# Gate stage of a hybrid encoder step: rows turned by VectorE, h added by accumulating loads, and rows finished one pair later

## The chip, the core and the metric

The kernel runs on one core of one Trainium2 chip. A core has five engines with their own instruction streams: TensorE (PE, its weight loads shown apart as PEld), VectorE (DVE), ScalarE (ACT), GpSimd (POOL) and SyncE (SP), which here only issues DMA transfers. POOL issues DMAs too, on a queue of its own. The metric is the device time of one launch in microseconds (us); lower is better. Traces give the span of one profiled execution from its first to its last instruction, and its own device time lies a little above that span.

## What is computed

2048 prompt frames and 32 frames of a running stream, D = 1024 channels in float32, go through one layer and a last norm:

```python
h = h + concat(yA, yB) @ w_out                       # "W_out stage"
gate = sigmoid(rmsnorm(h, g_ple) @ w_ple_gate)       # "gate stage"
h = h + (p @ w_ple) * gate
y = rmsnorm(h, g_final)                              # over the last axis, EPS = 1e-6
```

yA and yB come from one projection of rmsnorm(x), a short causal convolution and a multi-scale pooling; all of that lies ahead of the stages spoken of here and stays as it is. `rmsnorm(h, g)` is h / sqrt(mean(h*h) + EPS) * g. The kernel also returns states of the two mixers.

## The kernel before, in words

The program first makes yA and yB and leaves them in DRAM (`y_d`). The W_out stage reads them back, writes rows of h to DRAM (`h_d`) and the sums of squares of h to SBUF (`rs_h`, already turned into 1/rms). The product p @ w_ple is made beforehand for all but the very last tile and lies in DRAM (`e_d`). The gate weight, scaled by g_ple in `scale_gate` on ScalarE, lies in `g_d`.

The gate stage works on 17 row tiles: 16 of 128 prompt rows and a short one of 32. The short one goes first (`plain`), then eight pairs: seven in a loop, and `last_pair`, which has its own end. A pair is a 2 x 2 block product by a scheme of seven half-size products (`seven`): the left operand A is cut into A11, A12 (first tile of the pair, lower and upper half of the channels) and A21, A22 (second tile), with the sums S1 to S4 of them; the weight likewise (11, 12, 21, 22, T1 to T4). Each product is 12 matmuls, since float32 is carried as a high part and a low part in fp32r (hi*hi, hi*lo, lo*hi over four blocks of 128 channels). `split` makes the two parts: a cast on ScalarE, then a subtraction on VectorE. Three PSUM banks x, y, z of a pair hold the products, in this order: x 11, y 12, x S2, z S1, x S3, z S4, x 22. Between them `carry` copies the running sum of x or z out by ScalarE before the next product adds to it, and `out` turns a finished quarter into a gate: VectorE adds the carry, ScalarE takes the sigmoid with the row's 1/rms, VectorE multiplies by the tile e (L1324) and adds the result to the tile h (L1325).

While a pair runs, `prep_g` prepares A for the next one, in steps that are called between products. A needs channels on partitions, and `h_d` holds rows on partitions. Two ways stand in the code. `turned` (L1283) loads the rows as they are, ScalarE copies each half into another order of columns (L1291), TensorE turns it by four 128 x 128 transposes into PSUM (L1293). `turned_here` (L1297) loads the rows as blocks by four DMAs (L1302), and VectorE turns every 32 x 32 block in place (L1304). Before, the first tile of each pair goes the first way and the second tile the other. g_ple and the gate weight's rows are ordered to fit ("(q k c)").

When a pair's products are done, `done_g` (L1329) squares and sums a row on ScalarE (L88), makes 1/rms on POOL (L69, L73), scales on VectorE (L1332) and writes the rows to the output from POOL (L1333).

The order of instructions on each engine is set by a planner that sorts the program by estimated costs; `keep_in_program_order` ties an instruction to its place. Each engine works in order, so an instruction that waits holds up all behind it, DMA issues on SP and POOL too. Buffers come from rings (`tile_pool` with so many bufs): a new tile waits until the one that had its buffer is no longer read. Those that matter: `ya` (5 tiles of 128 x 1024: e, row loads), `xh` (3 of that size: h rows, gate weight rows), `qa` (before: 2 of 128 x 512), `ss` (3 of 128 x 512: the sums), `st` (4 of that size), `cmb` (8: the parts of A).

Of the kernel before, what the change touches and what calls it, by code (L numbers as in the profile page):

```python
# [22 lines left out]
PLE = 256  # L23
# [4 lines left out]
NH = D // 2  # L28
# [6 lines left out]
def trunk(ctx, tc, x_p, x_s, c_conv, c_pool, p_p, p_s, g_mix, w_in, conv_w, conv_b, pool_w,  # L35
# [271 lines left out]
    def ring4(t, name):  # L307
        return t.tile([P, D], F32, tag="t", name=name)
# [21 lines left out]
    with ExitStack() as s1:  # L330
# [17 lines left out]
        def put(piece, src):  # L348

            return split(piece[:, :, 0], piece[:, :, 1], src)  # L350
# [761 lines left out]
    with ExitStack() as s2:  # L1112
        pool = lambda name, bufs: s2.enter_context(tc.tile_pool(name=name, bufs=bufs, reuse_waits="tile"))
        w3, qa, xh, st, ss, cmb = (pool(*a) for a in (
            ("w3", 1), ("qa", 2), ("xh", 3), ("st", 4), ("ss", 3), ("cmb", 8)))

        def quarters(name, W):
            c = halves(slot(f"{name}_c"))
# [7 lines left out]
        def half_of(x, at, n=P):  # L1126
            return x[at[0]][:n, at[1] * NH:at[1] * NH + NH]
# [45 lines left out]
        def scale_gate(k):  # L1173

            ts = [qa.tile([P, NH], F32, tag="q", name=f"gs_{k}_{half}") for half in range(2)]
            rows = w_gate.rearrange("(q k c) n -> k q c n", q=4, k=KC)[k]
            for half, t in enumerate(ts):  # L1180
                nc.gpsimd.dma_start(t, rows[:, :, half * NH:half * NH + NH])
# [61 lines left out]
            next_gate()  # L1243


        def embedding_chunks(name):
            wp = []
            for k in range(2):
                raw = ring4(ya, f"{name}r_{k}")
# [33 lines left out]
        def turned(i):  # L1283

            r, n = tiles[i]
            t = load_rows(ya, "hn", i, h_d).rearrange("p (q k c) -> p k q c", q=4, k=KC)
            out = []
            for half in range(2):
                pt = tbank(f"pth_{i}_{half}")
                o = qa.tile([P, KH, P], F32, tag="q", name=f"ho_{i}_{half}")  # L1290
                nc.scalar.copy(o[:n].rearrange("p k (q c) -> p k q c", q=4), t[:n, half * KH:half * KH + KH])  # L1291
                for k in range(KH):
                    nc.tensor.transpose(pt[:, k * P:k * P + n], o[:n, k], ident[:n, :n])  # L1293
                out.append(pt.rearrange("p (k t) -> p k t", k=KH))
            return out

        def turned_here(i):  # L1297

            r, n = tiles[i]
            t = ring4(ya, f"hn_{i}")  # L1300
            for q in range(4):
                nc.sync.dma_start(t[q * 32:q * 32 + 32].rearrange("p (g c) -> p g c", g=4),  # L1302
                                  h_d[r:r + P, q * 256:q * 256 + 256].rearrange("(g p) c -> p g c", p=32))
            nc.vector.transpose(t, t)  # L1304
            u = t.rearrange("p (g k t) -> p k g t", g=4, k=KC)
            return u[:, :KH], u[:, KH:]

        def gate_ops(h, e, n, name, i):
            scale = lambda at: rs_h[:n, i + at[0]:i + at[0] + 1]

            def carry(ps, at):
                t = st.tile([P, NH], F32, tag="t", name=f"c_{name}_{at[0]}{at[1]}")
                nc.scalar.copy(t[:n], ps[:n])
                return t

            def out(ps, c, at):
                if c is None:
                    c = st.tile([P, NH], F32, tag="t", name=f"g_{name}_{at[0]}{at[1]}")
                    nc.scalar.activation(c[:n], ps[:n], AF.Sigmoid, scale=scale(at))
                else:  # L1320
                    nc.vector.tensor_tensor(c[:n], ps[:n], c[:n], op=ALU.add)
                    nc.scalar.activation(c[:n], c[:n], AF.Sigmoid, scale=scale(at))
                ee, hh = half_of(e, at, n), half_of(h, at, n)
                nc.vector.tensor_tensor(ee, ee, c[:n], op=ALU.mult)  # L1324
                nc.vector.tensor_tensor(hh, hh, ee, op=ALU.add)  # L1325

            return carry, out

        def done_g(i, h):  # L1329
            r, n = tiles[i]  # L1330
            rf = sumsq(h, n, f"f{i}")
            nc.vector.scalar_tensor_tensor(h[:n], h[:n], rf[:n], g_bc[:n], op0=ALU.mult, op1=ALU.mult)  # L1332
            nc.gpsimd.dma_start(rows_of(y_p, y_s, r, n), h[:n])  # L1333

        def short_ops(h, e, n):
# [17 lines left out]
        def last_pair(i, A):  # L1353
# [72 lines left out]
        def prep_g(i):  # L1426

            A = {}
            whole = lambda t: t.rearrange("p k (g t) -> p k g t", g=4)
# [7 lines left out]
                nc.vector.tensor_tensor(view(t), x, y, op=op)  # L1437
                return t

            lower = []  # L1440

            def first():
                lower.extend(turned_here(i + 1))

            def second():
                a21, a22 = lower
                s1 = comb("S1", a21, a22, ALU.add, whole)
                a11, a12 = turned(i)
                put("11", a11)
                s2 = comb("S2", s1, a11, ALU.subtract)  # L1450
                s3 = comb("S3", whole(a11), a21, ALU.subtract, whole)
                put("12", a12)
                put("S2", s2)
                s4 = comb("S4", a12, s2, ALU.subtract)
# [8 lines left out]
        S = {}  # L1463
        n = tiles[NT - 1][1]
        A = short("gl", turned(NT - 1), n)
        for step in prep_g(0).values():
# [5 lines left out]
        done_g(NT - 1, h)  # L1472
# [37 lines left out]
```

## Time and profile before

| | |
|---|---|
| median of 3 runs | 937.81 us (937.69 to 938.49) |
| the profiled execution: device time | 940.76 us |
| its span | 939.0 us |
| granted TensorE clock, mean | 0.992 |
| TensorE busy | 918.3 us, 98% of the span |
| VectorE busy | 727.4 us, 77% |
| ScalarE busy | 482.2 us, 51% |
| POOL busy | 129.3 us, 14% |
| gate stage, from the first pair's product to the end | 768.55 to 939.0 us |

How to read it: times are from the start of the span, in us unless marked ns. A group's line gives source line, engine, operation, output and input tile with shape, count, then busy time and the mean of one, then the idle time of the engine before it and what ended that. "The chain" is the work that ended last, followed back from the last instruction; each row is start, duration, engine, tile, line, count. Tile names are the program's; pth is the PSUM tile of the transposes, hn the row or block tile of h, ho the copy ahead of the transposes, g_S and g_fS the sums of A. Matmul durations overlap (389 ns each in a row, a new one every 227 ns).

### The profile page before, as it was taken

Reading aid. Unit: us, or ns where it says so; the run is one execution under the profiler, and the core shown is the slowest. Engines: PE = TensorE matmul, PEld = TensorE weight load, DVE = VectorE, ACT = ScalarE, POOL = GpSimd, SP = SyncE. Lnnn points to the kernel's source line nnn. Section 1 sums busy time; section 2 is a strip of 40 time slices with the busy share of each in tenths; the row PEclk is TensorE's granted clock in tenths of the full one; section 3 lists DMA queues with packets and bytes.
Section 4 is the critical chain, followed back from the end, with each engine's and each line's share of the span. In section 5 each row is a group of like instructions: output and inputs, shape, how many; then the busy total and the mean of one; then the engine's idle time right before and its main releaser. Section 6 shows DMA issues by size and latency. Waiting matters only on the chain.

```text
span 939.0 us, 13008 instructions
## 1 busy us (share of the span) xinstructions
PE 918.3 (98%) x4567; PEld 829.4 (88%) x4567; DVE 727.4 (77%) x1230; ACT 482.2 (51%) x894; POOL 129.3 (14%) x244
## 2 busy tenths in 40 slices
PE   6999999999999999999999999999999999999996
PEld 5899998999999999999999987888877868888885
DVE  6796898899588978685777589665554797888985
ACT  5653555464445554443444456334334875555663
POOL 2110232212000110000000010111211001211123
PEclk8999999999999999999999999999999999999998
DMA  8335556769955645427655359866785884566553
GB/s 240 85 121 175 154 146 203 222 174 297 417 167 139 180 142 166 129 71 272 195 167 175 128 187 289 270 181 183 218 244 171 318 264 129 206 220 244 183 207 113
DMA packets 133215, 182.97 MB, mean 195 GB/s; under 512 B 11164, under 2 KB 105116, under 8 KB 131869
## 3 DMA queue, kind: packets, MB, share of 16 engines
q1 hardware_dynamic: 117165, 131.70, 45.0%
q0 software_dynamic: 13248, 44.93, 14.6%
q10 hardware_dynamic: 2736, 5.51, 1.8%
q8 instruction: 36, 0.59, 0.3%
q14 instruction: 30, 0.25, 0.1%
HBM read 127.23 MB, written 54.86 MB: 194 GB/s over the span
## 4 chain that ended last, share of the span: by engine, by line
PE 79%; ACT 1%; DMA 1%; DVE 1%; POOL 0%; issue 0%; POOLq 0%; SPq 0%; ACTq 0%
PE x_o L167 9%; PE x_g L167 9%; PE x_zab L561 5%; PE x_ch L561 5%; PE x_zbv L561 5%; PE e L102 5%; PE z_g L167 5%; PE z_o L167 4%; PE z_ch L561 3%; PE z_zab L561 3%; PE z_zbv L561 2%; PE y_g L167 2%; PE y_o L167 2%; PE b L561 2%; PE za L561 2%; PE c L561 2%
## 5 line engine op out<-in xcount | busy, mean ns | idle before, releaser
L77 ACT CAST y_S<-y_fS 128x512 fp32r<-128x512 f32 x32 | 19.5, 621 | 43.1 <-PE x_o L167 19.4
L102 PE MATMUL e<-wq,pps 128*128 128x512 f32 (+1 forms) x156 | 38.8, 399 | 0.2 <-ACT pps L77 0.2
L406 DVE SCALAR_TENSOR_TENSOR xt<-xt,rstd_x,g_bc 128x1024 f32<-128x1024 f32 (+2 forms) x18 | 23.1, 1282 | 17.7 <-POOL rstd_x L73 17.5
L167 PE MATMUL x_g<-wg_b,g_S 128*128 128x512 f32 x128 | 35.9, 390 | 0.0
L167 PE MATMUL x_o<-wo_b,y_S 128*128 128x512 f32 x128 | 35.8, 391 | 0.0
L561 PE MATMUL x_zab<-B,w_zab_S 128*128 128x416 f32 x168 | 34.3, 352 | 0.5 <-ACT V L859 0.5
L561 PE MATMUL x_ch<-B,w_ch_S 128*128 128x416 f32 x168 | 34.6, 352 | 0.0
L561 PE MATMUL x_zbv<-B,w_zbv_S 128*128 128x416 f32 x168 | 34.4, 353 | 0.0
L561 PE MATMUL z_ch<-B,w_ch_S 128*128 128x416 f32 x168 | 34.1, 351 | 0.0
L561 PE MATMUL z_zbv<-B,w_zbv_S 128*128 128x416 f32 x168 | 34.1, 351 | 0.0
L561 PE MATMUL z_zab<-B,w_zab_S 128*128 128x416 f32 x168 | 34.0, 351 | 0.0
L102 PEld LDWEIGHTS e<-wq,pps 128*128 128x128 f32 (+1 forms) x156 | 27.4, 182 | 6.9 <-ACT pps L77 0.5
L561 PEld LDWEIGHTS x_zab<-B,w_zab_S 128*128 128x128 f32 x168 | 31.3, 188 | 1.1 <-ACT V L859 0.8
L561 PEld LDWEIGHTS x_zbv<-B,w_zbv_S 128*128 128x128 f32 x168 | 31.1, 188 | 0.8 <-ACT zs L859 0.4
L561 PEld LDWEIGHTS x_ch<-B,w_ch_S 128*128 128x128 f32 x168 | 31.2, 188 | 0.6 <-ACT c_s L859 0.3
L561 PEld LDWEIGHTS z_zab<-B,w_zab_S 128*128 128x128 f32 x168 | 31.4, 188 | 0.3
L561 PEld LDWEIGHTS z_ch<-B,w_ch_S 128*128 128x128 f32 x168 | 31.3, 188 | 0.4
L561 PEld LDWEIGHTS z_zbv<-B,w_zbv_S 128*128 128x128 f32 x168 | 31.3, 188 | 0.3
L69 POOL TENSOR_SCALAR ms_f<-ssq_f 128x1 f32<-128x1 f32 (+1 forms) x15 | 8.8, 588 | 160.7 <-ACT junk L88 160.7
L77 ACT CAST y<-y 128x512 fp32r<-128x512 f32 x24 | 14.8, 618 | 29.6 <-PE x_o L167 13.7
L1332 DVE SCALAR_TENSOR_TENSOR h<-h,rstd_f,g_bc 128x1024 f32<-128x1024 f32 (+1 forms) x15 | 19.3, 1284 | 12.7 <-POOL rstd_f L73 12.7
L167 PEld LDWEIGHTS x_o<-wo_b,y_S 128*128 128x128 f32 x128 | 24.0, 188 | 5.1 <-ACT c_o L1136 0.3
(571 smaller groups left out, 2670.4 us busy)
## 6 DMA issues: line engine op xcount, KB each, us to landing
y<-y_d SPq DMA_DIRECT2D x16, 512.0 KB, 12.8
x<-in_x_prompt_dram SPq DMA_DIRECT2D x16, 512.0 KB, 9.0
h_d<-x SPq DMA_DIRECT2D x16, 512.0 KB, 4.8
h<-h_d SPq DMA_DIRECT2D x16, 512.0 KB, 4.1
xt<-in_x_prompt_dram SPq DMA_DIRECT2D x15, 512.0 KB, 6.4
e<-e_d SPq DMA_DIRECT2D x15, 512.0 KB, 6.3
out_dram<-h POOLq DMA_DIRECT2D x14, 512.0 KB, 3.0
p_dT<-T POOLq DMA_DIRECT2D x12, 512.0 KB, 5.4
```

Source lines behind the costliest of these rows:

```text
L69: nc.gpsimd.tensor_scalar(ms[:n], ssq[:n], scalar1=1.0 / D, scalar2=EPS, op0=ALU.mult, op1=ALU.add)
L77: ins = nc.scalar.copy(hi, src)
L102: nc.tensor.matmul(ps[:n], pps[:, a, k, :n], wp[k][b][:, cs], start=k + q == 0, stop=k == 1 and q == 2)
L167: nc.tensor.matmul(ps[:n], lhs[:, k, a, :n], w[b][:, k], start=start and k + q == 0, stop=k == KH - 1 and q == 2, skip_group_check=True)
L406: nc.vector.scalar_tensor_tensor(xt[:n], xt[:n], r[:n], g_bc[:n], op0=ALU.mult, op1=ALU.mult)
L561: nc.tensor.matmul(ps[:, :NB], lhs[:, k, x], b[:, k, y], start=start and k + q == 0, stop=stop and k == KH - 1 and q == 2, skip_group_chec ...
L1332: nc.vector.scalar_tensor_tensor(h[:n], h[:n], rf[:n], g_bc[:n], op0=ALU.mult, op1=ALU.mult)
```

## The change

In the gate stage, for pairs two to eight, both tiles are loaded as blocks and turned by VectorE; the first pair's first tile still goes by TensorE. The block loads of the next pair are issued at the start of a pair, ahead of its loads of e. Their buffers are taken from `xh`, and from `qa` for every fourth tile. `qa` becomes one tile of 128 x 1024 instead of two of 128 x 512; in the W_out stage `scale_gate` takes the two halves of that tile.

The rows of h are no longer loaded in the loop. `out` ends with e times gate, and an accumulating DMA from POOL adds the rows of h from DRAM onto the tile e, half a tile at a time. So e becomes the new row, and it is finished one pair later: its sum of squares (`roots`) after the next pair's product z S1, its scaling and its output (`finished`) after x S3. The last pair still loads h, finishes the pair before it between its own products, and gets its buffers from `ss`, `xh` and `qa` instead of `ya`.

```diff
-            ("w3", 1), ("qa", 2), ("xh", 3), ("st", 4), ("ss", 3), ("cmb", 8)))
+            ("w3", 1), ("qa", 1), ("xh", 3), ("st", 4), ("ss", 3), ("cmb", 8)))
...
-            ts = [qa.tile([P, NH], F32, tag="q", name=f"gs_{k}_{half}") for half in range(2)]
+            gs = ring4(qa, f"gs_{k}")
+            ts = [gs[:, half * NH:half * NH + NH] for half in range(2)]
...
-        def turned_here(i):
+        def blocks(i):

             r, n = tiles[i]
-            t = ring4(ya, f"hn_{i}")
+            t = ring4(ya if i < 2 else qa if i % 4 == 1 else xh, f"hn_{i}")
             for q in range(4):
                 nc.sync.dma_start(t[q * 32:q * 32 + 32].rearrange("p (g c) -> p g c", g=4),
                                   h_d[r:r + P, q * 256:q * 256 + 256].rearrange("(g p) c -> p g c", p=32))
+            return t
+
+        def turned_here(t):
+
             nc.vector.transpose(t, t)
             u = t.rearrange("p (g k t) -> p k g t", g=4, k=KC)
             return u[:, :KH], u[:, KH:]
...
-                ee, hh = half_of(e, at, n), half_of(h, at, n)
+                ee = half_of(e, at, n)
                 nc.vector.tensor_tensor(ee, ee, c[:n], op=ALU.mult)
-                nc.vector.tensor_tensor(hh, hh, ee, op=ALU.add)
+                if h is None:
+                    r = tiles[i + at[0]][0]
+                    nc.gpsimd.dma_start(ee, h_d[r:r + P, at[1] * NH:at[1] * NH + NH], accum_op=ALU.add)
+                else:
+                    hh = half_of(h, at, n)
+                    nc.vector.tensor_tensor(hh, hh, ee, op=ALU.add)
...
-        def done_g(i, h):
+        def root_g(i, h, later=True):
+            return sumsq(h, tiles[i][1], f"f{i}", later=later)
+
+        def done_g(i, h, rf, later=True):
             r, n = tiles[i]
-            rf = sumsq(h, n, f"f{i}")
-            nc.vector.scalar_tensor_tensor(h[:n], h[:n], rf[:n], g_bc[:n], op0=ALU.mult, op1=ALU.mult)
+            ins = nc.vector.scalar_tensor_tensor(h[:n], h[:n], rf[:n], g_bc[:n], op0=ALU.mult, op1=ALU.mult)
+            if later:
+                tc.keep_in_program_order(ins)
             nc.gpsimd.dma_start(rows_of(y_p, y_s, r, n), h[:n])
...
-            pt = ring4(ya, "p_l")[:, :PLE]
+            pt = ss.tile([P, NH], F32, tag="s", name="p_l")[:, :PLE]
...
-            wp = embedding_chunks("wl")
+            wp = embedding_chunks("wl", (xh, qa))
...
-            seven(f"g{i}", A, W, carry, out, {5: lambda: second(1, NH)}, first_tile=True)
+            seven(f"g{i}", A, W, carry, out, {2: lambda: root(0), 3: lambda: (root(1), finished(0)), 4: lambda: finished(1), 5: lambda: second(1, NH)}, first_tile=True)
...
-            lower = []
+            rows = [blocks(i + b) for b in range(1 - here, 2)]
+            ready = []

             def first():
-                lower.extend(turned_here(i + 1))
+                ready.extend(turned_here(rows[0]))

             def second():
-                a21, a22 = lower
-                s1 = comb("S1", a21, a22, ALU.add, whole)
-                a11, a12 = turned(i)
-                put("11", a11)
...
+                if here:
+                    a11, a12 = ready
+                    put("11", a11, whole)
+                    a21, a22 = turned_here(rows[1])
+                    s1 = comb("S1", a21, a22, ALU.add, whole)
+                else:
+                    a21, a22 = ready
+                    s1 = comb("S1", a21, a22, ALU.add, whole)
+                    a11, a12 = map(whole, turned(i))
+                    put("11", a11, whole)
...
         for i in range(0, NT - 3, 2):
             A = S.pop(i)
-            h = [load_rows(xh, "h", i + b, h_d) for b in range(2)]
+            steps = prep_g(i + 2)
             e = [load_rows(ya, "e", i + b, e_d) for b in range(2)]
-            seven(f"g{i}", A, W, *gate_ops(h, e, P, f"g{i}", i), prep_g(i + 2))
-            for b in range(2):
-                done_g(i + b, h[b])
+            seven(f"g{i}", A, W, *gate_ops(None, e, P, f"g{i}", i), {**steps, 4: roots, 5: finished})
+            ready[:] = ([i + b, e[b]] for b in range(2))
         last_pair(NT - 3, S[NT - 3])
```

More of the change, by code (lines that the diff above doesn't have):

```diff
@@ L1287, in turned @@
             out = []
+            both = ring4(qa, f"ho_{i}").rearrange("p (h k t) -> p h k t", h=2, k=KH)
             for half in range(2):
                 pt = tbank(f"pth_{i}_{half}")
-                o = qa.tile([P, KH, P], F32, tag="q", name=f"ho_{i}_{half}")
+                o = both[:, half]
                 nc.scalar.copy(o[:n].rearrange("p k (q c) -> p k q c", q=4), t[:n, half * KH:half * KH + KH])
@@ L1422, in last_pair, with prep_g @@
             pps = embedded()
-            seven(f"g{i}", A, W, carry, out, {5: lambda: second(1, NH)}, first_tile=True)
+            seven(f"g{i}", A, W, carry, out, {2: lambda: root(0), 3: lambda: (root(1), finished(0)), 4: lambda: finished(1), 5: lambda: second(1, NH)}, first_tile=True)
             second(0, NH // 2)
-        def prep_g(i):
+        def prep_g(i, here=True):
             A = {}
@@ L1465, in trunk @@
         A = short("gl", turned(NT - 1), n)
-        for step in prep_g(0).values():
+        for step in prep_g(0, here=False).values():
             step()
@@ L1471, in trunk, with root, roots, finished @@
         plain("gl", A, W, n, *short_ops(h, e, n))
-        done_g(NT - 1, h)
+        done_g(NT - 1, h, root_g(NT - 1, h, False), False)
+        ready = []
+        def root(b):
+            ready[b].append(root_g(*ready[b]))
+        def roots():
+            for b in range(len(ready)):
+                root(b)
+        def finished(*bs):
+            for b in bs or range(len(ready)):
+                done_g(*ready[b])
         for i in range(0, NT - 3, 2):
             A = S.pop(i)
-            h = [load_rows(xh, "h", i + b, h_d) for b in range(2)]
+            steps = prep_g(i + 2)
             e = [load_rows(ya, "e", i + b, e_d) for b in range(2)]
-            seven(f"g{i}", A, W, *gate_ops(h, e, P, f"g{i}", i), prep_g(i + 2))
-            for b in range(2):
-                done_g(i + b, h[b])
+            seven(f"g{i}", A, W, *gate_ops(None, e, P, f"g{i}", i), {**steps, 4: roots, 5: finished})
+            ready[:] = ([i + b, e[b]] for b in range(2))
         last_pair(NT - 3, S[NT - 3])
```

12 lines of the change are left out of this document (6 added, 6 removed).

## The prediction

> **What bounds the kernel now.** I read the page first (busy times, the 40 slices), then the chain that ended last in order of time over the gate stage, then the busy times by stage, the groups of that stage, and its waits. The page:
>
> ```profile
> span 939.0 us, 13008 instructions
> PE 918.3 (98%) x4567; PEld 829.4 (88%) x4567; DVE 727.4 (77%) x1230; ACT 482.2 (51%) x894; POOL 129.3 (14%) x244
> PE   6999999999999999999999999999999999999996
> DMA  8335556769955645427655359866785884566553
> ```
>
> TensorE is busy in every slice but the first and the last, so a change pays only by what it takes off TensorE, or costs by what it makes TensorE wait for. The chain through the gate (start, us, line) shows what a pair of row tiles costs:
>
> ```profile
> 783.92 0.87 PE pth L1293 x8
> ...
> 785.94 5.44 PE x_g L167 x24
> ...
> 842.89 0.87 PE pth L1293 x8
> 843.76 2.06 PE z_g L167 x9
> 845.82 5.44 PE x_g L167 x24
> 851.26 2.72 PE y_g L167 x12
> 853.98 2.72 PE x_g L167 x12
> 856.70 2.72 PE z_g L167 x12
> 859.42 2.72 PE x_g L167 x12
> ...
> 901.55 0.87 PE pth L1293 x8
> ...
> 905.84 4.34 PE x_g L167 x19
> ```
>
> The chain never leaves TensorE: seven products of 12 matmuls, 2.72 us each, and one group of eight transposes (L1293), 0.87 us. From 785.94 to 905.84 lie six pairs and the last pair's transposes of p (0.22 us): (119.90 - 0.22) / 6 = 19.95 us a pair. Seven products are 7 x 2.72 = 19.05; 0.90 is left for the transposes with their seams. The stage and the tail (PE, PEld, DVE, ACT, POOL busy; clock; DMA share; GB/s):
>
> ```profile
> 785.90:905.84 119.94, 119.94 (x556) 99.75 (x555) 104.57 (x153) 69.64 (x122) 20.40 (x36) 1.00 0.59 205
> 905.84:939.00 33.16, 24.63 (x108) 19.82 (x107) 22.30 (x36) 16.40 (x31) 10.42 (x16) 0.91 0.32 120
> ```
>
> VectorE is at 104.57 / 119.94 = 87%, ScalarE at 58%, the DMA engines at 59%. No TensorE wait is in this window; what others wait for is small, or TensorE itself.
>
> **The change part by part.** Rows of the gate stage (count | busy us, mean ns):
>
> ```profile
> L1293 PE MATMUL pth<-ident,ho 128*128 128x128 f32 x48 | 6.4, 272 | 0.0
> L1291 ACT COPY ho<-hn 128x512 f32<-128x512 f32 x12 | 6.8, 622 | 0.0
> L77 ACT CAST g<-pth 128x512 fp32r<-128x512 f32 x12 | 6.5, 583 | 2.9 <-PE pth L1293 2.8
> L77 ACT CAST g<-hn 128x512 fp32r<-128x512 f32 x6 | 3.7, 618 | 0.0
> L1325 DVE TENSOR_TENSOR h<-h,e 128x512 f32<-128x512 f32 x24 | 15.9, 685 | 0.2
> L1304 DVE STREAM_TRANSPOSE hn<-hn 128x1024 f32<-128x1024 f32 x6 | 7.4, 1236 | 0.0
> L78 DVE TENSOR_TENSOR g_S<-g_fS,g_S 128x512 fp32r<-128x512 f32 x26 | 16.7, 681 | 0.2 <-ACT g_S L77 0.2
> L1332 DVE SCALAR_TENSOR_TENSOR h<-h,rstd_f,g_bc 128x1024 f32<-128x1024 f32 x12 | 15.4, 1285 | 10.0 <-POOL rstd_f L73 10.0
> L88 ACT ACTIVATE junk<-h 128x1024 bf16<-128x1024 f32 x12 | 12.7, 1058 | 11.5 <-DVE h L1325 7.4 <-issue 3.7
> L88 ACT ACTIVATION_READ_ACCUMULATOR junk<-h 128x1 f32 x12 | 2.2, 186 | 0.0
> ```
>
> *TensorE.* The eight transposes go for pairs two to eight, seven groups; nothing is added, and the products keep their order. They sit on the chain, so the gain is 7 x 0.90 = 6.3 us (7 x 0.87 = 6.1 by the rows alone); I take 6.2.
>
> *VectorE, a pair.* Four adds of h go (4 x 0.685 = 2.74 us), one STREAM_TRANSPOSE comes (1.24). Load: 17.43 - 2.74 + 1.24 = 15.9 of 19.05 us, 84%: no bound. *ScalarE.* Two copies go (1.24); two casts read SBUF instead of PSUM (+0.035 each). About 10.4 of 19.05 us.
>
> *The preparation moves earlier.* The new order finishes most of A for the next pair some 14 us before use, where L78 and L77 now finish parts within 3 us of it. These are off the path; without that cover the nearest was x 22, whose buffer VectorE must read within one 2.72 us product, as now.
>
> *Loads.* On SP two 512 KB row loads of h and one of hn leave a pair, four 128 KB block loads come, placed ahead of the e loads. On POOL four accumulating loads of 256 KB come: 28 more POOL instructions matter little at 17% busy, but each is queued in order with the rows' ms_f, rstd and output. Landing times of this stage, and the nearest row of POOL loading the same tile shape (in the stage of W_out, where DMA is busier):
>
> ```profile
> out_dram<-h POOLq DMA_DIRECT2D x12, 512.0 KB, 3.0
> h<-h_d SPq DMA_DIRECT2D x12, 512.0 KB, 4.1
> e<-e_d SPq DMA_DIRECT2D x11, 512.0 KB, 6.3
> hn<-h_d SPq DMA_DIRECT2D x24, 128.0 KB, 2.9
> ...
> L1181 POOL DMA_DIRECT2D gs<-in_w_ple_gate_dram x16: 690/747/753, 560.8 to 708.5; - x16
> ...
> DMA to landing us min/median/max: 6.6/8.9/12.0
> ```
>
> No accumulating load is in the trace, so its landing L has two ends: 3.0 us (a plain 512 KB from this queue) and 12.0 (the slowest gs). I take 6.5, the quick end of gs, since the gate's DMA share is 0.59, while the slices of the W_out stage in which gs is loaded (the 25th to the 30th of the DMA row) read 6 to 9. What waits for it: ScalarE's Square of the pair before (now after carry z), with every cast and copy of ScalarE behind it, and so TensorE's next PSUM carry.
>
> *How long L may be.* From the Square to the next accumulating load runs a fixed row of work: two Squares 2 x (1.06 + 0.19) = 2.5, cast of S4 0.62, then on VectorE six operations of 512 at 0.60 spacing (three L78 in a row take 1.88, row below), two L1332 at 1.2 and a STREAM_TRANSPOSE at 1.2: 3.1 + 7.2, with hand-overs about 10.5 us. One round must fit in a pair: 10.5 + 0.1 + L <= 19.05, so L up to 8.4 us costs nothing in the steady state; above it every pair grows by the excess, and above 9.3 a pair is longer than now (19.95).
>
> *The first pairs.* VectorE is later there (the blocks of tile 4 wait for the short tile's output); the first Squares leave about 7.5 us for L, and the carry of x in the third pair about 0.5 us of slack. Ends 0 and +1.5 (L = 9); taken +0.2.
>
> *The tail.* In the last pair three Squares now stand ahead of the copy of z that frees its PSUM sum for S4. Before (with the row that shows three L78 in 1.88 us, used above):
>
> ```profile
> 806.90 1.88 DVE L78 TENSOR_TENSOR g_S<-g_fS,g_S 128x512 fp32r<-128x512 f32 x3
> ...
> 919.51 0.59 ACT L1313 COPY c_g<-z_g 128x512 f32<-128x512 f32 x1 [1.12 <-PE z_g L167]
> 920.14 2.62 PEld L167 LDWEIGHTS z_g<-wg_d,g_S 128*128 128x128 f32 x12 [0.19 <-ACT c_g L1313]
> ```
>
> and its chain:
>
> ```profile
> 914.03 2.72 PE x_g L167 x12
> 916.75 2.72 PE z_g L167 x12
> 919.47 0.91 PE x_g L167 x4
> 920.38 2.83 PE z_g L167 x12
> ```
>
> After product y ends: add, sigmoid, product, add about 3.3 us, Square of half a row 0.8, two Squares 2.5, copy 0.6: 7.2 us. TensorE arrives after 2.72 + 2.72 + 1.36 = 6.8, so it waits about 0.5, and z S4 starts near 7.3 instead of 920.38 - 914.03 = 6.35. Half of that comes back, because only six instead of eight matmuls of S3 are left behind it. If L is above 6.3 us, the excess is added here whole. Ends -0.2 and +3; taken +0.7.
>
> *W_out's gs tile* is one buffer of the same size: both halves now wait for the later store, with a whole pair until use: nothing; ends 0 and +0.3.
>
> **Sum.** -6.2 + 0.2 + 0.7 = -5.3 us. The profiled execution took 940.76 us for its span of 939.0, so it would become 935.5; it lies 2.95 us above the median of the runs, 937.81, and from that the forecast is 932.5 us. Own range of this case: 931 to 935.
>
> [...]
>
> **The rivals.**
> 1. *Accumulating loads land late: slower.* Place: the Square's wait. From L = 9.3 on it decides. At L = 10 a pair takes 20.6: 6 x (20.6 - 19.95) = +3.9, less 0.9 for the first pair's group, plus 0.7 + 3.7 in the tail: 945 us. Against it: 3.0 and 4.1 us for twice the bytes; for it: 8.9 for gs, and a DMA share that rises. Packets explain that rise: blocks of 1 KB, not rows of 4 KB, and 2 KB for the accumulates. Chance 0.20, with L beyond. [...]
> 2. *L between 8.4 and 9.3:* at L = 9 a pair takes 19.6: -2.1 - 0.9 + 3.4 = +0.4, 938.2 us, no difference. Chance 0.07.
> 3. *VectorE stalls on blocks.* From the fifth pair on half of a tile's blocks stand on SP behind an e load that waits for a row output; about 7 us remain until the STREAM_TRANSPOSE, and e alone takes 6.3. A stall of 1 to 3 us in two pairs, partly covered by VectorE's 3.1 us of slack: 934 to 936.5. Chance 0.08.
> 4. *The transposes were free:* then nothing changes, 937.8. Against it: no wait of TensorE in the stage. Chance 0.03.
>
> **How the numbers follow.** Forecast 0.62. About 0.2% (1.9 us) is what a measurement of this kernel can tell. Faster: 0.62 + 0.08 = 0.70; same: 0.07 + 0.03 = 0.10; slower: 0.20. The range goes from 930.8 (full gain, tail at its lower end) to 943 (L about 9.8), leaving out some 0.12 above and 0.04 below.
>
> **What would show it.** Right: no pth matmuls after the first pair's own; pairs of 19.05 us in the chain; accumulating loads landing in 4 to 8 us; ScalarE's Square waiting under 1 us; a PE wait of about 0.5 us for the copy of z in the last pair. Wrong: "ACT junk <- DMA" among the long waits, PE waits for ScalarE's carries, pairs above 19.5 us, or STREAM_TRANSPOSE waiting for blocks.

## The result, and the profile after

The changed kernel takes 934.08 us (median of 6 runs, 931.75 to 935.53), the kernel before 938.10 us beside it (6 runs, 937.69 to 938.71): the ratio is 0.9953 with a 95% interval of 0.9939 to 0.9967. Two later sets of runs gave 0.9951 (0.9931 to 0.9970) and 0.9947 (0.9931 to 0.9964). The change makes the kernel 4.4 to 5.0 us faster by the ratios. The forecast was 932.5 us, a gain of 5.3.

The page of the profiled execution (device time 933.61 us) and its DMA slices:

```profile
span 931.8 us, 12938 instructions
PE 910.5 (98%) x4511; PEld 821.3 (88%) x4511; DVE 718.9 (77%) x1209; ACT 475.3 (51%) x880; POOL 147.1 (16%) x272
...
DMA  8255555759954645428655349765784885899892
```

TensorE is still the engine that is busy throughout. It runs 56 matmuls fewer, which are the seven groups of eight transposes, and is busy for 7.8 us less (918.3 before). In the five slices ahead of the last, the DMA engines went from 5 and 6 tenths to 8 and 9.

The span is 7.2 us shorter, more than the gain, because the two executions began differently. Work by stretch, in the same columns as in the prediction (PE, PEld, DVE, ACT, POOL busy; clock; DMA share; GB/s). The kernel before, with the first 80 us, the seven pairs (from the first pair's first product to the start of the product ahead of the last pair's y), and what lies behind them:

```profile
0.00:80.00 80.00, 70.97 (x353) 65.78 (x354) 63.64 (x116) 43.76 (x87) 13.03 (x55) 0.94 0.52 145
768.55:908.43 139.88, 139.88 (x648) 116.30 (x646) 120.73 (x177) 81.55 (x142) 21.71 (x39) 1.00 0.61 207
908.43:939.00 30.57, 22.04 (x97) 17.73 (x95) 19.70 (x32) 15.16 (x29) 10.42 (x16) 0.91 0.28 105
```

The changed kernel, between the same instructions:

```profile
0.00:80.00 80.00, 71.64 (x369) 66.35 (x370) 65.05 (x119) 44.91 (x88) 12.68 (x55) 0.98 0.54 153
766.24:900.22 133.98, 133.93 (x592) 110.29 (x590) 114.49 (x161) 75.46 (x128) 39.85 (x64) 1.00 0.84 210
900.22:931.80 31.58, 22.32 (x99) 17.84 (x96) 17.54 (x27) 14.47 (x28) 12.73 (x19) 0.93 0.44 138
```

The gate stage starts 2.3 us earlier (766.24 against 768.55) although nothing ahead of it is meant to be faster. What differs is the granted clock of the first 80 us, 0.98 against 0.94. It is an accident of the execution: over the runs below the stage starts anywhere from 764.0 to 769.0, at 767.8 or later in each of the five profiled executions that read 0.94 there (769.02 in the first order of the last pair; the first repeat, at 1.00, has 764.01). So the change is read from the start of the stage on. The seven pairs take 133.98 instead of 139.88 us, 5.9 less, and the end takes 31.58 instead of 30.57, 1.0 more: a gain of 4.9 us.

The pairs in the timeline of TensorE, one product of each row (start, us):

```profile
785.30 2.88 PE L167 MATMUL x_g<-wg_c,g 128*128 128x512 f32 x12
804.34 2.88 PE L167 MATMUL x_g<-wg_c,g 128*128 128x512 f32 x12
823.38 2.88 PE L167 MATMUL x_g<-wg_c,g 128*128 128x512 f32 x12
842.61 2.88 PE L167 MATMUL x_g<-wg_c,g 128*128 128x512 f32 x12
861.65 2.88 PE L167 MATMUL x_g<-wg_c,g 128*128 128x512 f32 x12
881.03 2.88 PE L167 MATMUL x_g<-wg_c,g 128*128 128x512 f32 x12
900.22 3.00 PE L167 MATMUL x_g<-wg_c,g 128*128 128x512 f32 x12
```

Pairs one, two, three and five take 19.04 to 19.06 us (the first from 766.24), the fourth 19.23, the sixth 19.38 and the seventh 19.19. The transposes of h are gone from them. Of the 0.6 us above seven times 19.05, 0.14 are the two transposes of p ahead of the last pair, which lie in the seven pairs before the change, too. The other 0.5 us are two short stalls of TensorE. The waits of this stage (760 to 932 us: engine, tile, line, waited for; us in total, times, longest):

```profile
DVE hn L1310 <- DMA hn<-h_d: 5.1, 3, 2.2
...
ACT junk L88 <- DMA e<-h_d: 3.1, 4, 1.1
...
PEld z_g L167 <- ACT c_g L1319: 0.6, 1, 0.6
...
PEld x_g L167 <- DVE c_g L1327: 0.5, 1, 0.5
...
PEld x_g L167 <- ACT c_g L1319: 0.3, 1, 0.3
PE z_g L167 <- ACT c_g L1319: 0.2, 1, 0.2
```

The first is STREAM_TRANSPOSE waiting for row blocks, the second ScalarE's Square waiting for accumulating loads. TensorE's weight loads wait three times. In the sixth pair (0.5 us, at 878.18) VectorE's add stands behind the STREAM_TRANSPOSE that waited 2.2 us for its blocks (876.31). In the fourth (0.3 us, at 828.85) ScalarE's copy stands behind work that a Square had delayed, which came 0.8 us late (818.11). The third, and the wait of the matmuls themselves, belong to the copy of z in the last pair. The loads that are added land in (issue row of the page, then the range):

```profile
e<-h_d POOLq DMA_DIRECT2D x28, 256.0 KB, 6.9
...
DMA to landing us min/median/max: 3.9/6.9/9.4
```

And the chain in the last pair, which begins with the second of the two Squares that stand ahead of the copy of z (its two instructions, the Square and the reading of its sum):

```profile
911.26 1.15 ACT junk L88 x2
912.41 0.48 ACT c_g L1319
...
912.94 3.01 PE z_g L167 x12
```

### The profile page after: what moved, and what is told of

It is laid out like the page before. It is cut to its first block, busy times and chain, and to the rows that moved or that the text cites. A ratio compares the mean times of both kernels' runs of the same rounds, so it can differ in the third digit from the quotient of the medians.

```text
span 931.8 us, 12938 instructions
## 1 busy us (share of the span) xinstructions
PE 910.5 (98%) x4511; PEld 821.3 (88%) x4511; DVE 718.9 (77%) x1209; ACT 475.3 (51%) x880; POOL 147.1 (16%) x272
## 5 line engine op out<-in xcount | busy, mean ns | idle before, releaser
L1333 POOL DMA_DIRECT2D e<-h_d x28 | 24.8, 907 | 53.3 <-DVE e L1330 40.4
L561 PEld LDWEIGHTS x_ch<-B,w_ch_S 128*128 128x128 f32 x168 | 31.2, 188 | 1.0 <-ACT c_s L859 0.7
L167 PEld LDWEIGHTS x_g<-wg_b,g_S 128*128 128x128 f32 x128 | 24.0, 188 | 5.0
```

The costliest lines, as they stand in the source:

```text
L167: nc.tensor.matmul(ps[:n], lhs[:, k, a, :n], w[b][:, k], start=start and k + q == 0, stop=k == KH - 1 and q == 2, skip_group_check=True)
L561: nc.tensor.matmul(ps[:, :NB], lhs[:, k, x], b[:, k, y], start=start and k + q == 0, stop=stop and k == KH - 1 and q == 2, skip_group_chec ...
L1333: nc.gpsimd.dma_start(ee, h_d[r:r + P, at[1] * NH:at[1] * NH + NH], accum_op=ALU.add)
```

## The experiments

### Is the gain the transposes' time on TensorE?

The changed kernel was run again, twice, beside its variants.

> The changed kernel itself, so that the variants are compared with it on one chip. Theory (the gain is the TensorE time of the seven groups of transposes, less about 1 us in the last pair): 933 to 935 us beside 937.8 to 938.7 of the kernel before, a gain of 3.5 to 5 us. Rival (part of the first measured gain was a lucky stretch ahead of the gate stage, where both kernels do the same work): a gain of 2 to 3 us. From the start of the first pair's first product to that of the last pair both say 134 us (139.9 before), seven pairs of 19.05 us and up to 0.7 us of short waits.

> The changed kernel once more, beside the two variants on one chip. Theory: 132.9 to 134.5 us from the first pair's first product to the last pair's, 31.5 us from there to the end, and a median 4 to 5 us below the kernel before. Rival (the tail's 31.5 us is an accident of two executions): a tail under 31 us.

Measured: 932.71 us beside 938.49, and 932.91 beside 937.55. In the two profiled executions the seven pairs take 133.44 us each, that is seven times 19.05 and 0.1 more, and what follows takes 31.55 and 31.60 us. The pairs in the first of them:

```profile
764.01:897.45 133.44, 133.44 (x591) 110.44 (x590) 115.00 (x161) 75.51 (x128) 39.43 (x64) 1.00 0.83 211
```

So without a stall the pairs gain 6.4 us, the end loses 1.0 in all three executions, and the whole is worth 5.4. A lucky stretch ahead of the stage, which was to leave a gain of 2 to 3 us, is ruled out: the ratios of the two sets give 4.6 and 5.0.

Then eight transposes that nobody needs were put back on TensorE in each pair:

```diff
             def first():
                 ready.extend(turned_here(rows[0]))
+                if here:
+                    pt = [tbank(f"idle_{i}_{c}") for c in range(2)]
+                    for c in range(8):
+                        nc.tensor.transpose(pt[c // 4][:, c % 4 * P:c % 4 * P + P], ident, ident)
```

> As changed, but in each of the seven pairs prepared by VectorE, TensorE also does eight transposes of the identity into the two PSUM banks of its old transposes; nothing reads them, and no other engine gets or loses work. Theory (the whole gain is TensorE time): 0.87 to 0.90 us a pair comes back, 6.1 to 6.3 us, so the time is 939 to 941 us, somewhat above the kernel before because the last pair's loss stays. Rival (the gain is rather that TensorE and ScalarE no longer wait for each other over the rows that are turned, so that bare transposes would fit into gaps): under 3 us comes back, 934 to 937.

Measured: 940.94 us, 1.0028 (1.0010 to 1.0046) of the kernel before, and 8.2 above the changed kernel beside it. The timeline shows 19.97 us for a pair that has them (785.57 to 805.54, to 825.50, 845.47 and 865.44), which is the 19.95 of before:

```profile
785.57 2.88 PE L167 MATMUL x_g<-wg_c,g 128*128 128x512 f32 x12
791.01 1.03 PE L1463 MATMUL idle<-ident 128*128 128x128 f32 x8
...
805.54 2.88 PE L167 MATMUL x_g<-wg_c,g 128*128 128x512 f32 x12
```

A group costs 0.93 us a pair, 6.5 in seven, whoever uses its result. The rest of the difference was, in this execution, a wait of 1.45 us for VectorE in the sixth pair, which lasts 1.75 us longer than its neighbours. The gain of the pairs is the time of the transposes on TensorE.

### Can the parts be had apart?

The turning alone: `before` with both tiles of a pair in blocks, h loaded and added by VectorE and rows finished in their own pair.

```diff
-            lower = []
+            rows = [blocks(i + b) for b in range(1 - here, 2)]
+            ready = []
...
-                a11, a12 = turned(i)
...
+                    a21, a22 = turned_here(rows[1])
```

> The turning alone: VectorE turns both tiles of pairs two to eight, but h is loaded as rows and added by VectorE, and rows are finished at the end of their own pair, all as before the change (the row blocks of both tiles lie in the e rows' buffers, where the row load and the blocks were). Theory (VectorE would have 17.43 + 1.24 = 18.7 us of work in a pair of 19.05, 98%, so that the accumulating loads are what makes room): TensorE waits for VectorE, pairs of 19.3 to 20.5 us, 934 to 942 us in all, no better than the changed kernel. Rival (98% is enough): pairs of 19.05 us with no loss in the last pair, 931.5 to 932.5 us, faster than the changed kernel by 1 to 2 us.

Measured: 935.11 us, 0.9970 (0.9955 to 0.9985) of before: half the gain. Pairs of 19.64 us from the third on, as the theory said. The end takes 31.2 us from 902.29, 0.6 more than before the change and 0.4 less than in the changed kernel, although no Square is moved: 0.14 of it are the transposes of p, which stand behind the mark here, S1 and S2 come late there too, and the last adds of h are slower (last section). VectorE in 785 to 895 us, and what the weight loads of one of these pairs waited for:

```profile
785.00:895.00 110.00, 109.82 (x473) 87.26 (x472) 103.60 (x147) 59.41 (x104) 26.28 (x36) 1.00 0.68 207
```

```profile
849.01 0.19 PEld L167 LDWEIGHTS x_g<-wg_a,g_S 128*128 128x128 f32 x1 [0.46 <-ACT g_S L77]
849.53 0.30 PEld L167 LDWEIGHTS z_g<-wg_a,g_S 128*128 128x128 f32 x2 [0.23 <-ACT g_S L77]
850.18 0.30 PEld L167 LDWEIGHTS x_g<-wg_a,g_S 128*128 128x128 f32 x2 [0.35 <-DVE g_S L78]
```

VectorE is busy for 94%, and the parts of S1 and S2, which TensorE multiplies right after y, are ready a few tenths after it wants them. TensorE is never idle for long, it is delayed by 0.6 us in each pair. So, with the turning by VectorE, the accumulating loads and the later finish are worth about 2 us (935.11 against 932.91 beside it). They take four adds a pair off VectorE, and S1 and S2 are ready in time; that the adds are the reason, and not the later finish, is argued, since no run has one without the other.

The other part alone: accumulating loads and the later finish, with the first tile of each pair turned by TensorE as before.

```diff
-            t = ring4(ya if i < 2 else qa if i % 4 == 1 else xh, f"hn_{i}")
+            t = ring4(ya if i < 2 else xh, f"hn_{i}")
...
-            steps = prep_g(i + 2)
+            steps = prep_g(i + 2, here=False)
```

> The accumulating loads and the finish a pair later alone: the first tile of every pair is turned by TensorE again, as before the change (the row blocks of the second tile then all lie in the x stage's buffers). Theory (the turning is the whole gain, the rest costs about 1 us in the last pair and nothing in the pairs): 19.95 us a pair again, 6.2 us above the changed kernel, 938.5 to 941 us, or 0 to 1.5 us above the kernel before. Rival (taking four adds of h off VectorE has a gain of its own): 934 to 937.

Measured: 978.36 us, 1.0428 (1.0399 to 1.0457). Neither theory is right. The waits from 764 to 905 us name another cause:

```profile
ACT ho L1293 <- DMA hn<-h_d: 16.4, 3, 7.9
PE pth L1295 <- ACT ho L1293: 15.3, 3, 7.4
```

The transposes wait for ScalarE's copies, and these for the row loads, which are issued late. A likely reason, not shown, is that such a row load takes its buffer from the ring of five that the rows e use, and these now stay in it for a pair longer; on SP's queue loads of e and of rows wait 24.5 us for finished rows to leave, but block loads on the same queue also wait 36.1 us for VectorE to have read their buffers (764 to 905 us). The price of the accumulating loads by themselves can't be read from this run.

### How late may the accumulating loads be?

The last accumulating load of a pair (second tile, first half) is issued twice, and the second one waits for the first (so this half gets h twice in the result):

```diff
-                    nc.gpsimd.dma_start(ee, h_d[r:r + P, at[1] * NH:at[1] * NH + NH], accum_op=ALU.add)
+                    for _ in range(1 + (at == (1, 0))):
+                        nc.gpsimd.dma_start(ee, h_d[r:r + P, at[1] * NH:at[1] * NH + NH], accum_op=ALU.add)
```

> As changed, but the pair's last accumulating load (second tile, first half) is issued twice, the second behind the first (this half gets h twice), so that what the Square waits for takes about 13.5 us instead of 6.8. The prediction's loop (Square to the next last accumulating load 10.5 us, and then L, must fit in 19.05 us): a pair takes about 24 us from the third on, 25 to 33 us in all, with 5 to 7 in the last pair besides, 965 to 975 us. Rival (there is no loop; a late Square only uses up ScalarE's own slack): pairs of 19 to 20.5 us, and 938 to 946 us in all.

Measured: 957.73 us, 1.0206 (1.0174 to 1.0238). That is slower than the rival allowed (938 to 946) and less slow than forecast (965 to 975). From 806.51 to 916.40 us five pairs take 22.0 us on average, one by one from 19.8 to 25.5. One round of the loop, from the timelines of ScalarE and POOL:

```profile
828.46 1.06 ACT L88 ACTIVATE junk<-e 128x1024 bf16<-128x1024 f32 x1 [4.76 <-DMA e<-h_d]
...
850.77 1.06 ACT L88 ACTIVATE junk<-e 128x1024 bf16<-128x1024 f32 x1 [3.31 <-DMA e<-h_d]
```

```profile
835.97 0.89 POOL L1334 DMA_DIRECT2D e<-h_d  x1 [0.65 <-DVE e L1330]
...
842.83 1.74 POOL L1334 DMA_DIRECT2D e<-h_d  x2 [4.24 <-DMA e<-h_d]
```

From the second tile's Square to its next accumulating load 7.5 us, 6.9 until that has landed, 7.9 until the second one has: 22.3 us for a round, and the pairs grow to it on average. The loop of the prediction exists and sets the pace once it is longer than a pair. Its fixed part is shorter for this load than I had it (7.5 from the second Square, where 10.5 less one Square gives 9.2). For the pair's last load to be issued, which is one of the first tile's, it is as forecast. In the first repeat of the changed kernel (ScalarE, POOL):

```profile
814.88 1.06 ACT L88 ACTIVATE junk<-e 128x1024 bf16<-128x1024 f32 x1
```

```profile
825.30 0.89 POOL L1333 DMA_DIRECT2D e<-h_d  x1 [0.85 <-DVE e L1330]
```

The first Square is followed by that load 10.4 us later.

Next the same 28 loads without the adding, so that the result lacks the product of e and the gate in 14 tiles:

```diff
-                    nc.gpsimd.dma_start(ee, h_d[r:r + P, at[1] * NH:at[1] * NH + NH], accum_op=ALU.add)
+                    nc.gpsimd.dma_start(ee, h_d[r:r + P, at[1] * NH:at[1] * NH + NH])
```

> As changed, but the 28 loads overwrite the product instead of adding to it (the output leaves the gated embedding out in the first 14 tiles): same bytes, same queue, same waits. Theory (adding makes a load count about twice on the DMA engines): over the pairs the DMA share falls from 0.84 to 0.6 to 0.7, the loads land in 3 to 5 us instead of 6.8, and the time falls by 0 to 1.5 us, because no Square then waits. Rival (the share rose because the row blocks have 1 KB packets): the share stays above 0.8 and the landing at 6 to 7 us.

Measured: 934.54 us, 0.9954 (0.9934 to 0.9973): no different from the changed kernel. The loads land in 5.4 us (median) where added ones take 6.9, and the DMA share, over 785 to 895 us, is 0.81. The rows are this kernel's, the changed kernel's, and that of the kernel before:

```profile
785.00:895.00 110.00, 109.34 (x482) 89.98 (x481) 92.79 (x130) 61.68 (x106) 26.41 (x55) 1.00 0.81 230
```

```profile
785.00:895.00 110.00, 109.95 (x485) 90.48 (x484) 93.02 (x132) 61.92 (x106) 34.65 (x56) 1.00 0.91 227
```

```profile
785.00:895.00 110.00, 110.00 (x507) 91.44 (x506) 96.56 (x142) 63.70 (x112) 17.24 (x32) 1.00 0.58 199
```

Of the rise, 0.23 stays without the adding, and 0.10 goes with it. Adding also lengthens what POOL spends on issuing one, 0.91 against 0.56 us (means of the groups). Neither shows in the time.

### What makes the scattered stalls?

Some executions show stalls of 0.3 to 3 us in single pairs. Three variants bear on them. The first turns the first pair's first tile on VectorE, too:

```diff
-        for step in prep_g(0, here=False).values():
+        for step in prep_g(0).values():
```

> As changed, but VectorE turns the first pair's first tile too, so no group of eight 128-row transposes is left on TensorE. Theory (each group on the chain costs 0.9 us): 0.9 us faster than as changed. Rival (VectorE is late in the first pair, between the short tile and the last embedding chunks, and its extra 1.24 us operation holds the first casts up): 0 to 1.5 us slower than as changed, with a TensorE wait ahead of the first pair's products.

Measured: 938.11 us, 1.0001 (0.9984 to 1.0019): the whole gain is lost, against both expectations (0.9 us faster, or at most 1.5 slower than as changed). The group is gone, and the pairs begin without a wait: from the first product of the W_out stage to the start of the gate stage this kernel takes 209.88 us, the changed one 210.79 to 210.85. The place of the loss is the fourth pair, in the timelines of ScalarE, VectorE and TensorE:

```profile
836.94 1.06 ACT L88 ACTIVATE junk<-e 128x1024 bf16<-128x1024 f32 x1 [2.65 <-DMA e<-h_d]
```

```profile
838.63 1.90 DVE L78 TENSOR_TENSOR g_S<-g_fS,g_S 128x512 fp32r<-128x512 f32 x3 [3.69 <-ACT g_S L77]
```

```profile
841.79 4.60 PE L167 MATMUL x_g<-wg_T,g 128*128 128x512 f32 x12 [2.75 <-DVE c_g L1327]
```

The planner had put VectorE's work in another order, so that the Square at 815.22 was followed by the last accumulating load only at 829.76, 14.5 us later. It landed in 7.2; a round of 21.7 us does not fit in 19.05. ScalarE's casts stand behind that Square, VectorE behind the casts, TensorE behind VectorE.

The second gives Squares and final products out one step later, the third only the final products (with a new order of the last pair, below):

```diff
-            seven(f"g{i}", A, W, *gate_ops(None, e, P, f"g{i}", i), {**steps, 4: roots, 5: finished})
+            seven(f"g{i}", A, W, *gate_ops(None, e, P, f"g{i}", i), {**steps, 5: roots, 6: finished})
```

```diff
-            seven(f"g{i}", A, W, *gate_ops(None, e, P, f"g{i}", i), {**steps, 4: roots, 5: finished})
+            seven(f"g{i}", A, W, *gate_ops(None, e, P, f"g{i}", i), {**steps, 4: roots, 6: finished})
```

> As changed, but in each pair the Squares and the final products of the pair before are given out one step later (behind the S3 product's output instead of ahead of it), which gives the accumulating loads some 3 us more. Theory (the stalls of 0.3 to 4 us that some executions show in a pair are Squares that wait for late accumulating loads): no wait for such a load, seven pairs within 133.7 us, and a median 0.5 to 1.5 us below the changed kernel's. Rival (the stalls come from row blocks and e rows that land late, because the row's buffer is freed still later now): the same stalls or longer ones, 0 to 3 us slower than as changed.

> As changed, but in each pair the final products of the pair before stand one step later (their Squares stay where they were), and the last pair is ordered as in the second attempt at the tail. Theory (the scattered stalls of the pairs are Squares that wait for accumulating loads at the end of the loop): the loop from a Square to the last accumulating load loses two final products, 2.4 us of 10.4, so no Square waits over 0.3 us, the seven pairs take at most 133.7 us, the stretch behind them 31.2, and the median is 0.5 to 1.5 us below the changed kernel's. Rival (the stalls come as much from row blocks that stand behind an e row's load, which waits for a finished row to leave its buffer; that buffer is freed 2.5 us later now): STREAM_TRANSPOSE waits for blocks 5 us or more in all, pairs of 134 us or more, and a median equal to the changed kernel's or above.

Measured: 935.41 us, 0.9974 (0.9953 to 0.9994), and 938.68 us, 1.0001 (0.9984 to 1.0018). Neither is faster than the changed kernel, the second is clearly slower, though no Square waits for an accumulating load in the first profile and only 0.3 us in the second. The waits of the second (764 to 935 us), and its queue on SP (785 to 900 us):

```profile
DVE hn L1310 <- DMA hn<-h_d: 9.1, 3, 5.0
...
PE x_g L167 <- DVE c_g L1327: 3.6, 2, 2.8
```

```profile
SPq L327 <- DMA out_dram<-e: 51.9, 7, 14.1
```

Loads of e (L327) wait for the finished rows to leave their buffers (51.9 us here, 51.4 in the first kernel, 43.8 as changed), row blocks stand behind them on SP's queue, and STREAM_TRANSPOSE waits for the blocks: 9.1 us, the longest 5.0, against 5.1, 1.7 and 3.9 in the three executions of the changed kernel. Seven pairs take 134.9 us in the first kernel and 139.0 in the second. So the change stands between two limits, each a few us away: order VectorE otherwise, and the Square's loop is too long (14.5 us and the landing, instead of 10.4); finish later, and the e rows' ring is freed too late. A finish earlier than in the change was not run.

### The last pair

Two orders of the last pair. In the first both Squares and both final products move behind the copy of z, in the second only the second tile's, and its final product goes behind the sums of S4 and S3.

```diff
-            seven(f"g{i}", A, W, carry, out, {2: lambda: root(0), 3: lambda: (root(1), finished(0)), 4: lambda: finished(1), 5: lambda: second(1, NH)}, first_tile=True)
+            seven(f"g{i}", A, W, carry, out, {4: lambda: (roots(), finished()), 5: lambda: second(1, NH)}, first_tile=True)
```

```diff
-            seven(f"g{i}", A, W, carry, out, {2: lambda: root(0), 3: lambda: (root(1), finished(0)), 4: lambda: finished(1), 5: lambda: second(1, NH)}, first_tile=True)
+            seven(f"g{i}", A, W, carry, out, {2: lambda: root(0), 4: lambda: (finished(0), root(1)), 5: lambda: (finished(1), second(1, NH))}, first_tile=True)
```

> As changed, but in the last pair both Squares of the pair before, with their roots and final products, are given out behind the copy of the z sum instead of ahead of it. Theory (the last pair's loss of 1.0 us is that copy waiting behind the Squares): z's S4 product starts 11.8 to 12.0 us after the last pair's first product instead of 12.7, the end comes 0.4 to 0.6 us earlier, and the time is that much lower. Rival (the loss is made up elsewhere, since the two products of the gate and e_l that follow have their own waits, or the two final products now stand in VectorE's way ahead of the S4 sum): no change of the end, or up to 1 us later.

> As changed, but in the last pair the second Square stands behind the copy of the z sum, and the second final product behind the sums of S4 and S3 on VectorE (in the first attempt at the tail both Squares had moved, and the two final products, which wait for the roots, stood ahead of those sums). Theory (the tail's loss is that copy, and the first attempt lost it again on VectorE): the S4 product starts about 12.0 us after the last pair's first product instead of 12.7, no wait of TensorE for VectorE behind it, and the end comes 0.3 to 0.5 us sooner: 31.0 to 31.2 us. Rival (the stretch behind the S4 product sets the end whatever stands ahead of it): 31.5 us or more.

Measured: 934.24 us, 0.9951 (0.9931 to 0.9970), and 934.03 us, 0.9963 (0.9947 to 0.9979); neither differs from the changed kernel within its interval. In the profiles the S4 product starts 11.90 us after the mark in both (12.72 as changed, 11.79 before). The first then loses it again: the final products stand ahead of the sum of S4.

```profile
919.08 1.28 DVE L1345 SCALAR_TENSOR_TENSOR e<-e,rstd_f,g_bc 128x1024 f32<-128x1024 f32 x1 [0.72 <-POOL rstd_f L73]
...
921.62 3.02 PE L167 MATMUL x_g<-wg_T,g 128*128 128x512 f32 x12 [0.29 <-DVE c_g L1425]
```

Its end is 32.4 us long. The second has 31.26 us (31.55 to 31.60 as changed), 0.3 less; it is right in the profile and too small for the runs to show. No variant beat the changed kernel.

## Why the prediction was right, point by point

- *TensorE, -6.2 us.* Right: 5.9 to 6.4 us less in the three executions, 0.93 us a group in the test that puts bare transposes back.
- *First pairs, +0.2.* Nothing was lost there: 19.06 and 19.04 us.
- *The tail, +0.7.* The mechanism was right, the size was 1.0. The S4 product starts 7.17 us after the end of product y (905.77 to 912.94; forecast 7.3, before 6.35). From the mark it is 0.93 later, and half is back by the last e_l product, 0.49, as said. The other 0.5 is the sum of three things that the step did not have. The last adds of h run beside a multiply of POOL and take 0.6 longer (rows below). From ScalarE's last product to the end of the span it takes 5.25 instead of 4.96 us, which stays unexplained. And VectorE's product of the last e_l and its gate no longer waits for ScalarE, which saves 0.4 (1.63 us from the start of e_l to it, before 2.00). That the errors of this step and of the one above nearly cancel in the sum (-5.3 forecast, -5.4 without stalls) is luck.
- *L, taken 6.5 us.* 6.9 and 6.8 (medians), 3.9 to 9.4. The loop, 10.5 us and L up to 8.4, held in the changed kernel's own order (10.4). Some landings are above 8.4, which the step, with one L for all loads, left out; these are the Square's waits of up to 1.1 us, where I had said under 1. That 6.5 was so near is in part luck: it was the quick end of the gs loads because the stage's DMA share was 0.59, and that share rose to 0.84.
- *VectorE, 84%.* 114.49 of 133.98 us, 85%.
- *The DMA share* rises as said, from 0.61 to 0.84 over the pairs. I gave blocks and half rows as the reason; most of it (0.23 of 0.33, on the window above) is indeed there without the adding. That the smaller packets are the reason is argued, since no run changes them alone. In the kernel before, the blocks (1 KB packets), alone on the DMA engines from 812.8 to 815.5 us, moved 194 GB/s at a share of 0.68, and rows of 4 KB, alone from 824.5 to 829, 331 GB/s at 0.92: by these two stretches a byte of the blocks took 1.26 times the share. Adding went with 0.10 of share and 1.5 us of landing (6.9 against 5.4); the added loads also came in smaller packets than the plain ones (15380 packets in all against 13695 from 766 to 905 us), which the run does not part from the adding. In that window POOL's queue has 41.3% of the DMA engines' time with the adding, 29.4% without it, and 11.9% in the kernel before, so that by an estimate from these shares the 28 loads took 1.7 times as long with it. POOL issues an accumulating load in 0.89 us (median; 0.85 to 1.21) beside a VectorE at 85%.
- *Rival 1, late loads:* the mechanism is real and was shown by making one load late (1.0206 of the kernel before) and by another order of VectorE; the changed kernel stays on the good side of it. *Rival 2, landings between 8.4 and 9.3 us:* not the rule, with a median of 6.9 and a longest of 9.4. *Rival 3, blocks:* 5.1 us of waits, the longest 2.2, all but 0.33 us covered (the sixth pair). I gave it 0.08 and 934 to 936.5 us; the first median, 934.08, lies in that range as well as in the forecast's, and it is the traces that tell them apart. It is the limit that the two later finishes ran into. *Rival 4, free transposes:* excluded.
- *W_out's single gs tile, 0.* Right: from the first product of that stage to the start of the gate stage it takes 210.93 us before (557.62 to 768.55) and 210.74 in the kernel with the turning alone, which both have the two old tiles, and 210.85, 210.81 and 210.79 in the three executions of the changed kernel.

The forecast from the median was 932.5, and the medians of the three sets are 934.08, 932.71 and 932.91. What stays open is 0.2 to 1.6 us. Runs of the changed kernel with the same mean clock, 0.996, differ by 6 us (930.83 and 936.85). The start of the gate stage alone differs by 2.2 us between its three profiled executions (764.01 to 766.24), all at 0.996. The stalls seen in the variants are of the size of the rest, but no profile of the changed kernel caught more than 0.5 us of them in all, so that they make this spread is argued and not shown.

## What to carry to other kernels

Read the gain of a step from the engine that sets the end: eight small transposes on a TensorE that never waits were worth just their own 0.93 us a pair. But whether another engine can take them depends on room in the right place: with 94% of VectorE busy half of the gain was lost to sums ready some tenths late, and the loads that took its adds away gave it back. When work is finished a round later, look for the two loops that this closes, the one through the data (Square, scaling, next load) and the one through the buffers (row out, row in, and what stands behind it in the queue), and keep both below a round with the slowest landing, not the median.

## What the runs showed of the hardware

A wait of TensorE of 2.75 us cost more than itself. In the kernel with the stall in the fourth pair the granted clock (the column behind the busy times) falls to one half some 0.9 us after TensorE goes on, for about 3.4 us, as the means of the stretches give it (those next to the half shown, 842.30 to 842.80 and 845.50 to 848.00, read 0.87 and 0.88):

```profile
841.79:842.30 0.51, 0.51 (x2) 0.47 (x3) 0.43 (x1) 0.51 (x2) 0.02 (x1) 1.00 0.00 0
...
842.80:845.50 2.70, 2.70 (x8) 2.04 (x8) 2.70 (x5) 0.93 (x2) 0.91 (x1) 0.50 0.02 6
```

The product of 12 matmuls took 4.60 us there, 1.7 more than 2.88; after a wait of 2.80 us in the kernel with the later final products it took 4.35, with the clock at 0.50 from 845.03 to 847.50, and after one of 1.45 us in the one with idle transposes 3.03, with the clock at 1.00 from 880.00 to 887.00.

In the changed kernel's end VectorE's two adds of h took 1.37 us beside a multiply of POOL:

```profile
922.99 1.27 POOL L1404 TENSOR_TENSOR hg<-h,g_bc 128x512 f32<-128x512 f32 x1
...
923.53 1.37 DVE L1398 TENSOR_TENSOR h<-h,g_l 128x256 f32<-128x256 f32 x2
```

In the kernel before, where that multiply had just ended, the same two took 0.75:

```profile
930.15 1.28 POOL L1389 TENSOR_TENSOR hg<-h,g_bc 128x512 f32<-128x512 f32 x1
...
931.62 0.75 DVE L1383 TENSOR_TENSOR h<-h,g_l 128x256 f32<-128x256 f32 x2
```

The 0.6 us are on the chain. Two other kernels show the same with more overlap. With the turning alone the adds start at 926.01 beside a multiply from 925.72 to 927.00 and take 1.61 us; in the first order of the last pair they start at 927.10 beside one from 926.74 to 928.02 and take 1.55. For 0.73, 0.99 and 0.92 us of overlap the adds are 0.62, 0.86 and 0.80 us longer than 0.75, so by these three VectorE does nearly nothing of them meanwhile. The two products of e_l and the gate just ahead of the adds (922.86), which have the same size and read one input from PSUM, take 0.76 us with the multiply beside them, no longer than the adds without it.
